# Adding the two halves of an attention result in memory: a tuned hybrid block kernel with accumulating transfers and a new order of units and steps

## The chip, the cores and the metric

The kernel runs on one core of a Trainium2 chip. The core has five engines with instruction queues of their own: TensorE (PE in the profile, with its weight loads shown as PEld), VectorE (DVE), ScalarE (ACT), GpSimd (POOL) and SyncE (SP). Sixteen DMA engines move data between memory and the core's SBUF. SP issues transfers through one hardware queue (q1 in the profile), GpSimd through a software queue (q0). The metric is the device time of one execution in microseconds, lower is better.

## The reference

One decoder layer over a sequence of 2048 tokens with model width 1024, in float32:

```python
h = rms_norm(x, norm_g)
u = jnp.einsum('bsd,dc->bsc', h, w_in)          # 8704 columns
v_c, b_c, c_c, z_c, q, k, v, z_a, gate_logits = jnp.split(u, SPLIT_POINTS, axis=-1)

y_c = b_c * causal_depthwise_conv(c_c * v_c, conv_w)     # width 3
y_c = y_c * jax.nn.silu(z_c)
y_a = jnp.einsum('bsc,cd->bsd', y_c, w_conv_out)

q = rms_norm(q.reshape(b, s, 16, 64), q_norm_g)
k = rms_norm(k.reshape(b, s, 4, 64), k_norm_g)
o = sliding_window_attention(q, k, v, sinks) * jax.nn.silu(z_a)   # window 128
y_b = jnp.einsum('bsc,cd->bsd', o, w_attn_out)

g_a, g_b = jnp.split(jax.nn.sigmoid(gate_logits + gate_b), 2, axis=-1)
merged = g_a * y_a + g_b * y_b
return x + jnp.einsum('bsd,de->bse', merged, w_out)
```

The attention result `o` has 1024 channels per token: 4 key heads, 4 query heads for each of them, 64 channels for each query head. It meets the gate `silu(z_a)` before its own projection.

## The kernel before

The sequence is worked in two halves ("tiles") of T = 1024 tokens, t = 0 and t = 1, channels on the 128 partitions and tokens along the free dimension. After both halves comes the last projection.

**Units.** A unit makes 256 output channels for the 1024 tokens of a half. It is the generator `sunit`: a block product of 2 x 2 by Winograd's scheme with seven products (`product`, L446) instead of eight. Every product is 12 matmuls of 128 x 128 by 128 x 512: each float32 operand is split into a high and a low part of the type that TensorE multiplies faster, and high x high, high x low and low x high are summed. The sums and differences of the weights and of the operands that the scheme needs are made by VectorE and ScalarE. A unit's name says what it makes: `q`, `k`, `v`; `cv` (C and V of the convolution branch), `b`; `ga`, `gb` (the merge gates); `z`, `za` (the gates of the two branches); `ya`, `yb` (the branches' own projections); `o` (the last one). Two units can run interleaved as a pair.

**Ticks.** The program is written out in order by hand. `run` advances one tick per product. `put(n, f)` registers a step for tick n; when that tick is reached, the step's instructions are written into the queues behind the product. A tick is thus a place in every engine's order, not a time: each engine takes its own instructions in that order and waits where an operand or a buffer is missing. A half counts 7 ticks for a unit and 14 for a pair. In the first half the key and value products take ticks 1 to 16, the `z` units begin at 186, the `za` units at 214, the `ya` pairs at 242.

**Attention.** A half has 32 rounds, one for each of 4 key heads and 8 blocks of 128 tokens, at the places in `AT0` and `AT1`. A round at place n loads queries and keys (n - 5), makes the scores in two PSUM banks of their own (`ps_s`), the exponentials (n + 1) and their norm (n + 2), turns the probabilities round through memory (`att_flip`, `att_back`), masks the two key blocks with GpSimd's affine selects (L1042, `att_low`, n + 10), and multiplies with the values (`att_values`, L1059, n + 13). The product `po` is a PSUM tile [128, 512]. Its upper and lower 64 partitions hold two halves of the same sums. In `att_out` (n + 14) ScalarE copies one half of `po` into a tile `o`, crosswise between partition halves (L1071); in `att_sum` (n + 15) VectorE adds the other half from PSUM (an `add`, recorded at L236), and SP stores the 128 x 256 result into `od[t]`, memory laid out as [8, 128, 1024]: channel group, channel in the group, token (L1079).

**The gates.** `fin_z` ends the `z` and `za` units. For each of the four pieces of a unit it loads 128 channels x 512 tokens of the branch's result (`load`, L1219: from `yd` for `z` into `zin`, from `od` for `za` into `zain`), ScalarE makes SiLU of the piece (L1229), VectorE multiplies it into the loaded tile, and the product is stored, with its sums and differences, for the `ya` and `yb` units (L1155 to L1163, L1236). `Z_AHEAD` says how many ticks ahead of its piece a load stands on SP.

**Next half.** `h_prep`, called ahead of the `z` units of the first half, makes the operands of the second: `x_roots` (L575) turns the roots of the token norms into rows with TensorE transposes, into a bank of the pool `ps_m` that holds also `po` and other small tiles; then GpSimd loads x, VectorE scales it, and the results are stored. `H_AT` gives the places. `w_prep` with `W_AT` does the like for the last weights. `load_set` loads what was stored, pair by pair, ahead of the units that use it.

**Buffers.** Nearly all tiles of up to 128 x 512 come from one pool of 19 slots (`big`); a tile's slot is free again when its last reader is done. Weights come through 4 raw tiles and 8 finished ones. `ps_m` has 3 PSUM banks, `ps_s` one tile of two banks.

Of the kernel before, what the change touches and what calls it, by code (L numbers as in the profile page):

```python
# [8 lines left out]
F32 = mybir.dt.float32  # L9
# [3 lines left out]
ALU = mybir.AluOpType  # L13
# [35 lines left out]
COL_GA, COL_GB = 6656, 7680  # L49

# [8 lines left out]

ORDER = (1, 5, 6, 2, 7, 3, 4)  # L60
# [13 lines left out]
AT1 = [  # L74
    41, 48, 54, 58, 67, 72, 75, 78, 81, 84, 88, 94, 98, 105, 109, 115, 119, 123, 126, 129, 132, 136,
    139, 142, 146, 150, 153, 157, 161, 164, 168, 174]
# [4 lines left out]
def block_kernel(  # L81
# [54 lines left out]
    od = [dram.tile([KC, P, T], F32, name=f"od{t}") for t in range(NT)]  # L136
# [434 lines left out]
    def x_roots(t, q, rs):  # L571

        pt = mbank(f"ptr{t}_{q}")
        for b in range(HB):
            nc.tensor.transpose(pt[:, b, :], rs[:, b : b + 1].to_broadcast([P, P]), ident)  # L575
# [488 lines left out]
    def att_out(t, j, b, po):  # L1064
        pov = po.rearrange("p (h e s c q) -> p h e s c q", h=2, e=2, s=2, c=2)
        o = slot([P, 2, P], F32, f"o{t}_{j}_{b}")
        parts = []
        for e in range(2):
            own, oth = HALVES[e], HALVES[1 - e]
            ov = o[own].rearrange("p c (h s q) -> p h s c q", h=2, s=2)  # L1070
            nc.scalar.copy(ov, pov[oth, :, e])  # L1071
# [140 lines left out]
    def fin_z(t, j, src, nm, key, to, at_of, eng):  # L1212
# [4 lines left out]
        def load(i, q):  # L1217
            o = got[i, q] = slot([P, H], F32, f"{nm}in{t}_{j}_{i}_{q}")
            nc.sync.dma_start(o, src[2 * j + i, :, hs(q)])  # L1219
# [120 lines left out]
    def h_prep(t, n0):  # L1340
# [4 lines left out]
        def roots(q):  # L1345
            rb[q] = x_roots(t, q, st["rt"][q])
# [32 lines left out]
    for t in range(NT):  # L1379
# [6 lines left out]
        def two(key, c0, t, j0):  # L1386
            paired.update((len(plan), len(plan) + 1))
            for j in range(j0, j0 + 2):
                at_((key, t, j), c0 + j * UC)

        if t == 0:
            for i in range(2):
                plan.append(("R", wkv[i * H : (i + 1) * H], ("kv", i)))
        else:
            two("ga", COL_GA, t, 0)
            at_(("k", t), COL_K)
            at_(("v", t), COL_VV)
        for j in range(NKV):
            at_(("q", t, j), COL_Q + j * UC)
            if t == j == 0:  # L1400
                plan[-1] = ("P",) + plan[-1][1:]
        for k in range(KC):
            s(("cv", t, k), (w_in2, COL_C + k * P), (w_in2, COL_V + k * P))
            if k % 2:
                at_(("b", t, k // 2), COL_B + (k // 2) * UC)
        for j in range(2 if t else 0, NJ):
            at_(("ga", t, j), COL_GA + j * UC)
        for j in range(NJ):
            at_(("gb", t, j), COL_GB + j * UC)
        for j in range(NJ):  # L1410
            at_(("z", t, j), COL_Z + j * UC)
        for j in range(NJ - 2):
            at_(("za", t, j), COL_ZA + j * UC)
        two("za", COL_ZA, t, NJ - 2)
        for key, w in (("ya", w_co), ("yb", w_ao)):
            for j in range(NJ):
                if j % 2 == 0:
                    paired.update((len(plan), len(plan) + 1))
                s((key, t, j), (w, j * UC), (w, j * UC + P))
# [92 lines left out]
    put(2, lambda: stats(0, 0))  # L1512
    put(2, lambda: stats(0, 2))
    put(2, lambda: roots(0))
    put(6, lambda: turned(0))
    put(7, lambda: stats(1, 0))
    put(7, lambda: stats(1, 2))
    put(8, lambda: roots(1))
    put(12, lambda: turned(1))
    put(4, lambda: plain_op(0, 1))  # L1520
    put(5, lambda: plain_op(2, 1))
    put(5, lambda: plain_op(4, 1))
    put(5, lambda: plain_op(6, 1))
    put(5, lambda: plain_op(1, 1))
    put(4, lambda: plain_op(3, 1))
    put(6, lambda: plain_op(5, 1))
    put(6, lambda: plain_op(7, 1))
    put(6, lambda: norm_l(0, 0, st))
    put(7, lambda: norm_l(0, 2, st))
    put(8, lambda: norm_l(0, 4, st))  # L1530
    put(6, lambda: norm_l(0, 6, st))
    put(9, lambda: norm_l(0, 1, st))
    put(8, lambda: norm_l(0, 3, st))
    put(7, lambda: norm_l(0, 5, st))
    put(6, lambda: norm_l(0, 7, st))
    put(9, lambda: form(0, 1, 0, st))
    put(15, lambda: form(0, 1, 1, st))
    put(8, lambda: form(0, 1, 2, st))
    put(14, lambda: form(0, 1, 3, st))
    put(12, lambda: norm_r(0, 0, st))  # L1540
    put(15, lambda: norm_r(0, 2, st))
    put(15, lambda: norm_r(0, 4, st))
    put(15, lambda: norm_r(0, 6, st))
    put(15, lambda: form(0, 8, 0, st))
    put(15, lambda: form(0, 8, 1, st))
    put(17, lambda: form(0, 8, 2, st))
    put(16, lambda: form(0, 8, 3, st))
    put(15, lambda: first_sum(0, st))
    put(16, lambda: first_sum(1, st))
    put(19, lambda: first_sum(2, st))  # L1550
    put(16, lambda: first_sum(3, st))
    put(16, lambda: form(0, 5, 0, st))
    put(17, lambda: form(0, 5, 1, st))
    put(20, lambda: form(0, 5, 2, st))
    put(17, lambda: form(0, 5, 3, st))
    put(13, lambda: norm_r(0, 1, st))
    put(15, lambda: norm_r(0, 3, st))
    put(12, lambda: norm_r(0, 5, st))
    put(14, lambda: norm_r(0, 7, st))
    put(19, lambda: second_sum(0, st))  # L1560
    put(17, lambda: second_sum(1, st))
    put(21, lambda: second_sum(2, st))
    put(19, lambda: second_sum(3, st))
    put(23, lambda: form(0, 6, 0, st))
    put(18, lambda: form(0, 6, 1, st))
    put(22, lambda: form(0, 6, 2, st))
    put(21, lambda: form(0, 6, 3, st))
    put(10, lambda: form(0, 2, 0, st))
    put(11, lambda: form(0, 2, 1, st))
    put(14, lambda: form(0, 2, 2, st))  # L1570
    put(9, lambda: form(0, 2, 3, st))
    put(20, lambda: third(1, st))
    put(16, lambda: third(3, st))
    put(22, lambda: third(5, st))
    put(21, lambda: third(7, st))
    put(26, lambda: form(0, 7, 0, st))
    put(22, lambda: form(0, 7, 1, st))
    put(24, lambda: form(0, 7, 2, st))
    put(27, lambda: form(0, 7, 3, st))
    put(23, lambda: t4(0))  # L1580
    put(22, lambda: t4(1))
    put(21, lambda: t4(2))
    put(23, lambda: t4(3))
    put(15, lambda: form(0, 3, 0, st))
    put(17, lambda: form(0, 3, 1, st))
    put(17, lambda: form(0, 3, 2, st))
    put(16, lambda: form(0, 3, 3, st))
    put(29, lambda: form(0, 4, 0, st))
    put(24, lambda: form(0, 4, 1, st))
    put(26, lambda: form(0, 4, 2, st))  # L1590
    put(29, lambda: form(0, 4, 3, st))
    KV_AT = {"p": (8, 9, 17, 19), "v": (8, 11, 19, 36), "r": (14, 32), "b": (29, 25, 39, 39)}
# [54 lines left out]
    for t in range(NT):  # L1647
# [3 lines left out]
        if t > 0:  # L1651
            paired_units([(("ga", t, j), ops, fin_g(t, 0, j)) for j in range(2)])
        a0 = t0 + (14 if t else 0)
        attention(t, [a0 + n for n in (AT0, AT1)[t]])
        if t > 0:
            run(sunit(("k", t), ops, fin_k(t)))
            run(sunit(("v", t), ops, fin_v(t)))
        for j in range(NKV):
            if t == j == 0:
                run(qunit(("q", t, j), ops, fin_q(t, j)))  # L1660
            else:
                run(sunit(("q", t, j), ops, fin_q(t, j), t == 0 and j < Q_TWO))
        for k in range(KC):
            run(sunit(("cv", t, k), ops, fin_cv(t, k, ys)))
            if k % 2:
                run(sunit(("b", t, k // 2), ops, fin_b(t, k // 2, ys)))
        if t + 1 < NT:
            h_stats(t + 1, tick[0] + 2)
        for j in range(2 if t else 0, NJ):
            run(sunit(("ga", t, j), ops, fin_g(t, 0, j)))  # L1670
        for j in range(NJ):
            run(sunit(("gb", t, j), ops, fin_g(t, 1, j)))
        if t + 1 < NT:
# [88 lines left out]
```

## Time and profile before

| | |
|---|---|
| runs | 1908.94, 1909.58, 1904.54 us; median 1908.94 |
| profiled execution | 1909.62 us, span 1907.9 us, granted clock 0.999 |
| busy | PE 1888.2, DVE 1591.0, ACT 1002.2, POOL 658.3 us |
| instructions | 28039 |
| DMA | 426.36 MB, 243141 packets, mean 223 GB/s |

The span runs from the first to the last instruction. Busy is the time in which at least one instruction of an engine was at work; matmuls overlap each other by more than a third, so a group's mean of 390 ns is not its step of 227 ns. "A <- B: t, n, m" in a list of waits means that A waited for B t us in all, n times, m us at the longest. A transfer's time "to landing" runs from its issue to its completion. SPq and POOLq stand for the engines' queues; a transfer that waits for a buffer waits there, with everything behind it on the same queue.

### The profile page before, as it was taken

To read this page: it belongs to the slowest core of one execution; us is meant where nothing else is said; L and a number is where in the kernel's file an instruction comes from. 1 tells how busy PE (TensorE), PEld (TensorE's weight loads), DVE (VectorE), ACT (ScalarE), POOL (GpSimd) and SP (SyncE) were. 2 spreads that over 40 slices of the span, in tenths; PEclk is the share of its full clock that TensorE was granted. 3 is DMA by queue.
4 is the path that set the end of the run, shared out by engine and by line. 5 is a ranking of instruction groups with operands and counts; after the bars stand their busy time and mean duration, and the time that the engine had idled before them with its cause. 6 is when DMAs were issued, how large, how long until landed. Compare 5 with 4: busy or idle time off the path is not lost.

```text
span 1907.9 us, 28039 instructions
## 1 busy us (share of the span) xinstructions
PE 1888.2 (99%) x8654; PEld 1566.9 (82%) x8654; DVE 1591.0 (83%) x2708; ACT 1002.2 (53%) x1990; POOL 658.3 (35%) x958
## 2 busy tenths in 40 slices
PE   9999999999999999999999999999999999999999
PEld 7778888888888888878887788888888888888887
DVE  7989899899887889887579989989888879887654
ACT  7655544567666345345445645555666436434321
POOL 1372444355665111121056344534665311111000
PEclk9999999999999999999999999999999999999999
DMA  8385554579876878999368556557887769989653
GB/s 305 98 221 161 174 169 149 170 236 289 246 233 213 281 263 307 322 291 303 113 185 200 159 166 194 162 174 211 245 251 225 268 218 349 331 263 279 227 174 111
DMA packets 243141, 426.36 MB, mean 223 GB/s; under 512 B 32240, under 2 KB 106992, under 8 KB 242992
## 3 DMA queue, kind: packets, MB, share of 16 engines
q1 hardware_dynamic: 202848, 314.13, 49.9%
q0 software_dynamic: 40000, 110.41, 20.3%
q8 instruction: 69, 1.13, 0.2%
q14 instruction: 80, 0.66, 0.1%
q10 hardware_dynamic: 144, 0.03, 0.0%
HBM read 278.43 MB, written 146.01 MB: 222 GB/s over the span
## 4 chain that ended last, share of the span: by engine, by line
PE 83%; DVE 6%; DMA 5%; issue 3%; POOL 2%; ACT 1%; SPq 0%; DVEq 0%; POOLq 0%; ACTq 0%
PE Y L446 28%; PE Vcv L446 4%; PE Xcv L446 4%; PE Xgb L446 2%; PE Xz L446 2%; PE Vz L446 2%; PE Vgb L446 2%; PE Xo L446 2%; PE Xza L446 2%; PE Vo L446 2%; PE Vza L446 2%; PE po L1059 2%; PE Xb L446 2%; PE Vb L446 2%; PE Xga L446 2%
## 5 line engine op out<-in xcount | busy, mean ns | idle before, releaser
L1021 POOL DMA_DIRECT2D x<-fd x256 | 139.7, 552 | 92.6 <-DMA fd<-f 60.3
L1042 POOL TENSOR_SCALAR_AFFINE_SELECT xh<-xh 64x512 fp32r<-64x512 f32 x64 | 69.3, 1082 | 141.6 <-DVE xl L236 98.7
L1014 POOL DMA_DIRECT2D fd<-f x64 | 36.9, 577 | 222.1 <-DVE f L236 180.6
L994 ACT ACTIVATE p<-s,st,rq 128x128 f32<-128x128 f32 x256 | 112.8, 449 | 0.0
L446 PE MATMUL Xcv<-oph,wcv_ah 128*128 128x512 f32 x256 | 79.4, 391 | 0.0
L1042 POOL TENSOR_SCALAR_AFFINE_SELECT xl<-xl 64x512 fp32r<-64x512 f32 x64 | 66.6, 1040 | 4.4
L1269 POOL DMA_DIRECT2D md<-thyb x32 | 27.5, 874 | 100.7 <-DVE thyb L236 95.9
L1042 POOL TENSOR_SCALAR_AFFINE_SELECT yp<-xl 64x512 fp32r<-64x512 f32 x64 | 57.4, 897 | 3.1
L1042 POOL TENSOR_SCALAR_AFFINE_SELECT yp<-yp 64x512 fp32r<-64x512 f32 x64 | 55.3, 864 | 4.2
L328 ACT CAST wcv_sh<-wcv_raw 128x1024 fp32r<-128x1024 f32 x16 | 16.8, 1053 | 74.3 <-DVE wcv_raw L236 68.9
L446 PEld LDWEIGHTS Xcv<-oph,wcv_ah 128*128 128x128 f32 x256 | 47.5, 188 | 9.5
L236 DVE TENSOR_TENSOR o<-po,o 64x256 f32<-64x256 f32 x128 | 53.4, 417 | 1.2
L816 POOL DMA_DIRECT2D q2d<-q_h x64 | 44.2, 690 | 26.4 <-ACT q_h L811 18.8
L236 DVE SCALAR_TENSOR_TENSOR y<-u,cols,y 128x512 f32<-128x512 f32 x64 | 50.5, 789 | 3.1 <-ACT y L1108 1.8
L236 DVE TENSOR_TENSOR opa<-ina,opa 128x512 fp32r<-128x512 f32 x56 | 36.2, 686 | 18.5 <-ACT opa L263 18.2
L991 ACT ACTIVATE st<-st 128x4 f32<-128x4 f32 x64 | 13.1, 205 | 72.4 <-DVE st L236 71.9
L994 ACT ACTIVATION_READ_ACCUMULATOR p<-s,st,rq 128x1 f32 x256 | 50.6, 198 | 0.0
L816 POOL DMA_DIRECT2D q2d<-q_l x64 | 44.1, 689 | 17.6 <-DVE q_l L236 8.7
L236 DVE TENSOR_TENSOR p<-p,st 128x512 f32<-128x512 f32 x64 | 47.4, 741 | 3.2
L1071 ACT COPY o<-po 64x256 f32<-64x256 f32 x128 | 47.0, 367 | 6.0 <-PE po L1059 3.7
L446 PE MATMUL Xcv<-oph,wcv_al 128*128 128x512 f32 x128 | 49.9, 389 | 0.0
L236 DVE TENSOR_TENSOR opc<-inc,opc 128x512 fp32r<-128x512 f32 x56 | 36.1, 686 | 14.4 <-ACT opc L263 14.3
(761 smaller groups left out, 6653.5 us busy)
## 6 DMA issues: line engine op xcount, KB each, us to landing
wcv_raw<-in_w_in SPq DMA_DIRECT2D x32, 512.0 KB, 3.9
q<-q2d SPq DMA_DIRECT2D x64, 256.0 KB, 4.3
v<-vd SPq DMA_DIRECT2D x128, 128.0 KB, 3.6
fd<-f POOLq DMA_DIRECT2D x64, 256.0 KB, 3.5
x<-fd POOLq DMA_DIRECT2D x256, 64.0 KB, 3.1
gd<-th SPq DMA_DIRECT2D x64, 256.0 KB, 3.1
wq_raw<-in_w_in SPq DMA_DIRECT2D x16, 512.0 KB, 5.1
q2d<-q_h POOLq DMA_DIRECT2D x64, 128.0 KB, 4.5
```

Source lines behind the costliest of these rows:

```text
L236: r = f(*args, **kw)
L328: return (lambda: nc.scalar.copy(hi, src), lambda: vec.tensor_tensor(out=lo, in0=src, in1=hi.bitcast(F32), op=ALU.subtract))
L446: nc.tensor.matmul(ps, lhsT=w[:, j, :], rhs=b[:, m, :], start=start and j == 0 and i == 0, stop=j == KP - 1 and i == 2, skip_group_check=n ...
L816: nc.gpsimd.dma_start(q2d[t][j][half, q * 2 * HB : (q + 1) * 2 * HB, i, e, :], src[HALVES[e]].bitcast(F32).rearrange("p (b x) -> p b x", x ...
L991: nc.scalar.activation(out=st[:, 3], in_=st[:, 2], func=AF.Exp)
L994: nc.scalar.activation(out=p[:, i, :], in_=sg[:, i, HD : 3 * HD], func=AF.Exp, bias=st[:, 1, i : i + 1], scale=rv[:, i // 2, i % 2 : i % 2 ...
L1014: nc.gpsimd.dma_start(fd, f)
L1021: nc.gpsimd.dma_start(x[QUADS[k]], src[k])
L1042: nc.gpsimd.affine_select(out=d4, in_=s4, pattern=[[0, 2], [-32 * sg, 2], [0, G], [-sg, 32]], compare_op=ALU.is_gt if prev else ALU.is_ge, ...
L1059: nc.tensor.matmul(po[:, cs], lhsT=v2[:, kind, :], rhs=xx[:, :, h * HD : (h + 1) * HD], start=h == 0 and n == 0, stop=n == 2, skip_group_c ...
L1071: nc.scalar.copy(ov, pov[oth, :, e])
L1269: nc.gpsimd.dma_start(md[t][k, :, hs(q)], m, accum_op=ALU.add)
```

## The change

The change has four parts.

1. **Attention result.** `att_out` now copies both halves of `po` into a tile `o` of [128, 2, 2, 128], each on its own partitions, two copies of [128 x 256]. VectorE adds nothing. `att_sum` stores the lower 64 partitions through SP into `od`, and `ADD_WAIT` = 2 ticks later GpSimd issues a transfer of the upper 64 partitions that adds to the same bytes. `od` is laid out anew: [4 key heads, 64 channels, 2 (e), 2 (c), 1024 tokens]. The gate's load reads 128 channels out of it with the order of dimensions e, channel, token.
2. **Roots.** For the second half both transposed rows of roots go into one tile of the scores' pool `ps_s` instead of two banks of `ps_m`; they stand 5 ticks later.
3. **Order of units.** It is given by two lists of names, `SEQ0` and `SEQ1`. The units are the same, as are the pairs.
4. **Places.** Steps at the start, some attention rounds, the first group of `H_AT` and of `W_AT` and `Z_AHEAD` (2 to 1) are placed anew.

```diff
+OP_X = [-1, 2, 2, 6, 7, 7, 8, 12]
+OP_P = [5, 4, 5, 4, 5, 6, 5, 6]
...
+SEQ0 = (
+    "q0 q1 q2 q3 cv0 cv1 cv2 cv3 b0 cv4 cv5 b1 b2 cv6 cv7 b3 gb1 ga0 gb2 ga1 gb0 ga2 ga3 gb3 z0 "
+    "z1 z2 z3 za0 za1 za2+za3 ya0+ya1 ya2+ya3 yb0+yb1 yb2+yb3")
+SEQ1 = (
+    "ga0+ga1 k v q0 q1 q2 cv0 q3 cv1 cv2 b0 cv3 ga3 b1 cv4 cv5 b2 cv6 cv7 gb1 b3 ga2 gb2 gb3 "
+    "gb0 z0 z1 z2 z3 za0 za1 za2+za3 ya0+ya1 ya2+ya3 yb0+yb1 yb2+yb3")
...
-Z_AHEAD = 2
+Z_AHEAD = 1
...
-H_AT = (11, 26, 66, 80)
-W_AT = [15, 33, 67, 84]
+H_AT = (16, 26, 66, 80)
+W_AT = [18, 33, 67, 84]
+ADD_WAIT = 2
...
-    51, 56, 61, 66, 72, 78, 82, 87, 93, 99, 103, 108, 113, 119, 123, 127, 130, 135, 139, 142, 146, 149,
-    153, 156, 160, 163, 167, 170, 174, 177, 181, 184]
+    51, 56, 62, 66, 72, 78, 82, 87, 93, 99, 103, 108, 113, 119, 123, 127, 130, 135, 139, 142, 146, 149,
+    153, 156, 160, 163, 166, 170, 174, 177, 181, 184]
...
-    od = [dram.tile([KC, P, T], F32, name=f"od{t}") for t in range(NT)]
+    od = [dram.tile([NKV, HD, 2, 2, T], F32, name=f"od{t}") for t in range(NT)]
...
     def att_out(t, j, b, po):
         pov = po.rearrange("p (h e s c q) -> p h e s c q", h=2, e=2, s=2, c=2)
-        o = slot([P, 2, P], F32, f"o{t}_{j}_{b}")
-        parts = []
+        o = slot([P, 2, 2, P], F32, f"o{t}_{j}_{b}")
         for e in range(2):
-            own, oth = HALVES[e], HALVES[1 - e]
-            ov = o[own].rearrange("p c (h s q) -> p h s c q", h=2, s=2)
-            nc.scalar.copy(ov, pov[oth, :, e])
-            parts.append((ov, pov[own, :, e]))
-        return o, parts
-
-    def att_sum(t, j, b, got):
-        o, parts = got
-        for ov, pv in parts:
-            add(ov, pv, ov)
-        nc.sync.dma_start(
-            od[t][2 * j : 2 * j + 2, :, b * P : (b + 1) * P].rearrange("c p q -> p c q"), o)
+            nc.scalar.copy(o[:, e].rearrange("p c (h s q) -> p h s c q", h=2, s=2), pov[:, :, e])
+        return o
+
+    def att_sum(t, j, b, o):
+        to = od[t][j, :, :, :, b * P : (b + 1) * P].rearrange("d e c q -> d (e c) q")
+        nc.sync.dma_start(to, o[LH].rearrange("p e c q -> p (e c) q"))
+        put(tick[0] + ADD_WAIT, lambda: nc.gpsimd.dma_start(to, o[UH].rearrange("p e c q -> p (e c) q"), accum_op=ALU.add))
...
-            nc.sync.dma_start(o, src[2 * j + i, :, hs(q)])
+            nc.sync.dma_start(o, src(2 * j + i, q))
...
-            rb[q] = x_roots(t, q, st["rt"][q])
+            if q == 0:
+                rb["banks"] = ps_s.tile([P, 2, HB, P], F32, tag="s", name=f"ptr{t}")
+            rb[q] = x_roots(t, q, st["rt"][q], rb["banks"][:, q])
...
+            elif key == "z":
+                fin = fin_z(t, j, lambda k, q: yd[t][k, :, hs(q)], "z", ("c", t), ycd[t], at_of, nc.sync)
+            elif key == "za":
+                fin = fin_z(t, j, lambda k, q: od[t][k // 2, :, :, k % 2, hs(q)].rearrange("d e q -> e d q"), "za", ("a", t), ocd[t], at_of, nc.gpsimd)
```

More of the change, by code (lines that the diff above doesn't have):

```diff
@@ L1384, in at_ @@
             s(key, (w_in2, c0), (w_in2, c0 + P))
[L1386 to L1389, printed above, removed]
         if t == 0:
@@ L1393, in block_kernel @@
                 plan.append(("R", wkv[i * H : (i + 1) * H], ("kv", i)))
[L1394 to L1419, printed above, removed]
+        for word in (SEQ0, SEQ1)[t].split():
+            both_ = word.split("+")
+            for name in both_:
+                if len(both_) > 1:
+                    paired.add(len(plan))
+                key, j = name.rstrip("0123456789"), int(name[-1]) if name[-1].isdigit() else None
+                if key in ("ya", "yb"):
+                    w = w_co if key == "ya" else w_ao
+                    s((key, t, j), (w, j * UC), (w, j * UC + P))
+                elif key == "cv":
+                    s((key, t, j), (w_in2, COL_C + j * P), (w_in2, COL_V + j * P))
+                elif j is None:
+                    at_((key, t), COLS[key])
+                else:
+                    at_((key, t, j), COLS[key] + j * UC)
+                if t == 0 and name == "q0":
+                    plan[-1] = ("P",) + plan[-1][1:]
     for n in range(S // P // 2):
@@ L1567, in block_kernel @@
[L1567 to L1592, printed above, removed]
+    for n, f in zip(OP_X, (
+            lambda: stats(0, 0), lambda: stats(0, 2), lambda: roots(0), lambda: turned(0),
+            lambda: stats(1, 0), lambda: stats(1, 2), lambda: roots(1), lambda: turned(1))):
+        put(n, f)
@@ new lines, in block_kernel, with forms, each, rights @@
+    for c in (0, 2, 4, 6, 1, 3, 5, 7):
+        put(OP_P[c], lambda c=c: plain_op(c, 1))
+    for c in (0, 2, 4, 6, 1, 3, 5, 7):
+        put(OP_L[c], lambda c=c: norm_l(0, c, st))
+    def forms(i):
+        for j in range(KP):
+            put(OP_F[KP * i + j], lambda j=j: form(0, FORMS[i], j, st))
+    def each(i, f):
+        for j in range(KP):
+            put(OP_S[KP * i + j], lambda j=j: f(j))
+    def rights(p):
+        for j in range(KP):
+            put(OP_R[2 * j + p], lambda c=2 * j + p: norm_r(0, c, st))
@@ L1593, in block_kernel @@
+    forms(0)
+    rights(0)
+    forms(1)
+    each(0, lambda j: first_sum(j, st))
+    forms(2)
+    rights(1)
+    each(1, lambda j: second_sum(j, st))
+    forms(3)
+    forms(4)
+    each(2, lambda j: third(2 * j + 1, st))
+    forms(5)
+    each(3, t4)
+    forms(6)
+    forms(7)
+    KV_AT = {"p": OP_K[:4], "v": OP_K[4:8], "r": OP_K[8:10], "b": OP_K[10:]}
     kv = KV()
@@ L1663, in block_kernel @@
[L1663 to L1666, printed above, removed]
-        if t + 1 < NT:
[L1668 to L1673, printed above, removed]
-            h_prep(t + 1, tick[0])
-        else:
-            w_prep(tick[0])
@@ new lines, in block_kernel @@
+        if t + 1 < NT:
+            h_stats(t + 1, tick[0] + STATS_AT)
+        for word in (SEQ0, SEQ1)[t].split():
+            n = tick[0] + 1
+            if word == "z0":
+                (h_prep if t + 1 < NT else w_prep)(*((t + 1,) if t + 1 < NT else ()), tick[0])
+            if word == "za2+za3":
+                load_set(("c", t), n, opa)
+            if word == "ya2+ya3":
+                load_set(("a", t), n, opb)
+            if word == "yb2+yb3":
+                load_set(("h", t + 1) if t + 1 < NT else ("w", 0), n, x_state(t + 1)["ops"])
+            names = word.split("+")
+            if len(names) > 1:
+                paired_units([
+                    unit_of(name, lambda e, i=i, n=n: n + 2 * e + i) for i, name in enumerate(names)])
+            elif t == 0 and word == "q0":
+                run(qunit(("q", 0, 0), ops, fin_q(0, 0)))
+            else:
+                run(sunit(*unit_of(word, lambda e, n=n: n + e)))
```

123 lines of the change are left out of this document (32 added, 91 removed).

## The prediction

> **What bounds the kernel now.** I read the page first: busy times and the chain that ended last. Then the stretches by stage, then who TensorE (PE) waited for, then the rows of the instructions and transfers that the diff names.
>
> ```profile
> span 1907.9 us, 28039 instructions
> ...
> PE 1888.2 (99%) x8654; PEld 1566.9 (82%) x8654; DVE 1591.0 (83%) x2708; ACT 1002.2 (53%) x1990; POOL 658.3 (35%) x958
> ...
> PE 83%; DVE 6%; DMA 5%; issue 3%; POOL 2%; ACT 1%; SPq 0%; DVEq 0%; POOLq 0%; ACTq 0%
> ```
>
> TensorE is the bound: it idles 1907.9 - 1888.2 = 19.7 us in all. The change leaves every matmul in place, so what it can win lies inside those 19.7 us; what it can lose has no such limit. The stretches below (columns: length, busy time of PE, PEld, DVE, ACT, POOL with counts, clock, mean busy share of the 16 DMA engines, GB/s) say where the idle time is.
>
> ```profile
> 0.00:100.00 100.00, 93.96 (x411) 75.81 (x411) 86.28 (x173) 68.65 (x121) 29.34 (x56) 0.98 0.62 202
> 100.00:415.00 315.00, 313.43 (x1463) 261.06 (x1463) 285.53 (x531) 169.67 (x379) 137.53 (x199) 1.00 0.60 179
> 415.00:480.00 65.00, 63.99 (x309) 53.61 (x308) 60.22 (x143) 47.96 (x110) 38.34 (x54) 1.00 0.88 283
> 985.00:1310.00 325.00, 320.54 (x1488) 265.42 (x1487) 293.54 (x538) 180.72 (x403) 151.40 (x217) 1.00 0.63 181
> 1750.00:1908.00 158.00, 154.15 (x681) 127.32 (x679) 89.10 (x121) 42.13 (x59) 3.43 (x4) 1.00 0.55 174
> ```
>
> Start and tail hold 6.0 + 3.8 us. The stretches with attention in them (100 to 480 and 985 to 1310) hold 1.6 + 1.0 + 4.5 = 7.1 us; VectorE is 90% busy in them. PE's longest single waits:
>
> ```profile
> PE ptr L575 <- DVE rtok L569: 2.2, 1, 2.2
> PE Y L446 <- DVE Vcv L236: 2.1, 1, 2.1
> ...
> PE po L1059 <- POOL xl L1042: 1.4, 1, 1.4
> ```
>
> So 7.1 us is all that a lighter VectorE and better places could return there, and 2.2 us at the first roots.
>
> **The change, part by part.**
>
> ```profile
> L1269 POOL DMA_DIRECT2D md<-thyb x32 | 27.5, 874 | 100.7 <-DVE thyb L236 95.9
> ...
> L236 DVE TENSOR_TENSOR o<-po,o 64x256 f32<-64x256 f32 x128 | 53.4, 417 | 1.2
> ...
> L1071 ACT COPY o<-po 64x256 f32<-64x256 f32 x128 | 47.0, 367 | 6.0 <-PE po L1059 3.7
> ```
>
> and of the transfers (issues, KB each, median us from issue to landing):
>
> ```profile
> od<-o SPq DMA_DIRECT2D x64, 128.0 KB, 2.6
> ...
> zain<-od SPq DMA_DIRECT2D x32, 256.0 KB, 5.6
> ...
> md<-thyb POOLq DMA_DIRECT2D x32, 256.0 KB, 7.0
> ```
>
> VectorE loses 128 additions of 417 ns, 53.4 us. ScalarE keeps 128 copies, on 128 partitions instead of 64 with the same 256 elements each: 0. The PSUM bank comes free after the copy, one addition sooner. All this is beside PE. Its worth on the path is between 0 and the 7.1 us above; the waits there are shared between VectorE, ScalarE and GpSimd (POOL), so I take half, -3.5.
>
> The store keeps 128 KB on SP. New are 64 accumulating transfers on POOL. The nearest row is the accumulation into md, 0.874 us of POOL each: 64 x 0.874 = 56 us more in stretches where POOL is about 45% busy (151.40 of 325.00). Each waits for its store to land. The store is issued two ticks earlier; a tick is one product of 12 matmuls, 2.72 us by this row of the chain (24 matmuls):
>
> ```profile
> 693.87 5.44 PE Xza L446 x24
> ```
>
> Two ticks are 5.4 us against a landing of 2.6, so the usual wait is 0. Behind the waiting accumulation stand the next rounds' affine selects (L1042) and transfers, and PE's po products wait for those selects. I take 0; the dear end is the second rival. Nothing excludes a gain by the freer bank, which is in the -3.5. The slot of o is held until the accumulation has landed: 5.4 + 0.9 + 7.0 instead of 2.6, 10.7 us more, 64 times over some 700 us of attention stretches, about one slot of 19; taken as 0, at worst it delays SP's loads by the like of the first rival's small waits.
>
> The gated read of the attention result (zain<-od) is where I see the cost. Before, one read takes a [128 x 512] block whose 128 rows lie evenly in memory. After, the od layout is [4, 64, 2, 2, 1024], and the read walks "e d q": an outermost dimension of 2 (the halves e), then 64 rows, then 512 contiguous elements, into 128 partitions. How a transfer of such a shape is dealt out to the DMA engines no row of before shows, because every transfer there has at least 32 entries outermost on both sides, and all ran on 16 engines:
>
> ```profile
> DMA packets 243141, 426.36 MB, mean 223 GB/s; under 512 B 32240, under 2 KB 106992, under 8 KB 242992
> ...
> q1 hardware_dynamic: 202848, 314.13, 49.9%
> ...
> q10 hardware_dynamic: 144, 0.03, 0.0%
> ```
>
> Queue q10 carried one transfer, the constants: 128 rows and 16 more packets, one completion per engine. Of the 32240 short packets 128 are those rows, and the other 32112 are 16 for each of 2007 transfers. So the price has two ends. Dealt to 16 engines, the read costs what it costs now. Dealt by its outermost entries, it has two shares, and two engines carry all of it. The stage rows, from the first zain load's issue to its last use in each half of the sequence, and the loads themselves:
>
> ```profile
> 663.90:744.70 80.80, 80.46 (x355) 66.10 (x354) 70.03 (x100) 40.02 (x64) 15.77 (x30) 1.00 0.77 275
> 1531.00:1610.50 79.50, 79.50 (x352) 65.63 (x351) 68.34 (x97) 39.25 (x63) 14.29 (x27) 1.00 0.75 268
> ```
>
> One busy engine moves 275 / (16 x 0.77) = 22.3 GB/s here (268 / (16 x 0.75) gives the same). A 262144-byte read over 16 engines takes each 0.73 us; over two it takes each 5.87 us. A half has 16 such reads: 93.9 us of both engines instead of 11.7. That alone is longer than the stage. Other traffic keeps an engine busy for 0.77 x 80.8 - 11.7 = 50.5 us of the first stage and 0.75 x 79.5 - 11.7 = 47.9 us of the second. Three values:
> - nothing of it stands before the reads: 93.9 - 80.8 = 13.1 and 93.9 - 79.5 = 14.4, +27.5 us;
> - all of it: 63.6 + 62.3, +125.9 us;
> - the part on SP's own queue, 314.13 of 426.36 MB or 74%, which is served in the order of issue, stands in the way and POOL's does not: 93.9 + 37.3 - 80.8 = 50.4 and 93.9 + 35.4 - 79.5 = 49.8, +100 us.
>
> Between the 16-engine end (0) and these I take two engines, since two shares is what the read's own shape offers without regrouping it, and the third value, since the reads and three quarters of the traffic are one queue. The delay reaches PE: VectorE multiplies zain in its program order, and its additions for PE's next products stand behind. What slack there is, these rows show:
>
> ```profile
> 663.86 1.29 SPq L1219 DMA_DIRECT2D zain<-od  x1
> ...
> 665.87 2.70 SPq L1219 DMA_DIRECT2D zain<-od  x3
> ...
> 670.34 0.69 DVE L236 TENSOR_TENSOR zain<-zain,zas 128x512 f32<-128x512 f32 x1 [0.38 <-DMA zain<-od]
> ...
> 681.18 0.69 DVE L236 TENSOR_TENSOR zain<-zain,zas 128x512 f32<-128x512 f32 x1
> ```
>
> Four loads go out in 4.7 us and are used between 6.5 and 17.3 us after the first; on two engines they alone need 4 x 5.87 = 23.5. Already now the first use waits 0.38 us. With Z_AHEAD 1 each load stands one tick (2.7 us) later on SP, behind a store or a weight load more.
>
> [...]
>
> The rest. The roots of the next half go into the score banks: the same 8 transposes, at ticks 201 and 202 counted from the start, when the last scores (tick 185) are read; no PE wait on these roots is among those of before, so 0 (dear end: one bank wait like the 2.2 above). The h loads, five ticks later in their first group, and the w_out loads, three later, keep more than 60 ticks to the sets that read them: 0. The order of units keeps their number, and so PE's work; cv units between lighter ones spread VectorE's load (in the -3.5), while y tiles wait longer for their b unit, 8 of 19 slots instead of 4 before b0: from -7.1 with the gain above to a wait or two of 2.1, taken 0. Start steps move by one to three ticks: between -2.2 and +2.2, taken 0.
>
> Sum: 1909.6 (the profiled execution: 1907.9 and 1.7 around it) + 100 - 3.5 = 2006 us. The median of the runs, 1908.94, is 0.7 below that execution.
>
> **The rivals.**
> - *The read is spread over all 16 engines.* Place: the zain loads; then they land in about 5.6 us within the 6.5 to 17 of slack, and PE stays the bound. 1909.6 - 3.5 = 1906, between 1902.5 and 1912 (one VectorE wait of 0.4 per load in six). For it: nothing in the trace binds a transfer to its outermost dimension. Against: all of its 2007 transfers fit that rule as well. It decides if a load's landing stays under 6.5 us. Faster or no change.
> - *POOL becomes the late engine.* Accumulations wait for stores that land late, and hold back the affine selects. If one round in four costs PE what POOL's worst select did, 16 x 1.4 = +22: 1909.6 + 22 - 3.5 = 1928. For it: transfers in the busier stages, reads of 256 KB though, land later than two ticks, as the row below shows. Against: POOL is idle more than half of the attention stretches. It decides when stores land later than 5.4 us.
>
> ```profile
> thyb<-gd SPq DMA_DIRECT2D x32, 256.0 KB, 8.7
> ```
>
> **How the numbers follow.** Two engines 0.72, with its own range 1934 (+27.5 - 3.5) to 2036 (+125.9); spread 0.21; POOL 0.07. I put the first that high because both layouts of the read are known exactly, the stage has no room (0.77 busy), and the only way out is a regrouping that nothing shows. About 0.3% (5.7 us) is what a measurement of this kernel can tell from no change; the three runs of before span 5.0. Spread gives 0.09 faster, 0.10 the same, 0.02 slower; the others are slower. The range goes from 1903, which takes in two thirds of the spread case and POOL, to 2036: 0.14 + 0.07 + 0.65 = 0.86.
>
> **What would show it.** In the profile after: the count of packets under 512 B. The 64 new transfers add 64 x 16 = 1024; at two completions for each of 32 reads 448 are missing, 32816, while 33264 means 16 engines and the forecast is wrong. zain<-od landing at 12 us or more in the median against 5.6; VectorE waiting for zain by some 100 us in all, PE idle about 60 us in each of the two gate stages and ya beginning that much later; DMA share lower there than 0.77. VectorE busy 53 us less, POOL 56 us more. POOL waits on o's landing, and PE's waits for xl growing past 1.4 us, would show the second rival. Waits of 3 us each could also lower the granted clock, which is 0.98 in the first stretch with its waits and 1.00 in all others; then the loss is above my range.

## The result and the profile after

The changed kernel takes 2004.14 us in the median (2002.12 to 2004.89), the kernel before 1909.35. The ratio is 1.0499, 95% interval 1.0483 to 1.0514. Predicted were 2006 us. The page of the changed kernel, in the lines shown of before, with the group of VectorE's gate products and that of the new transfers:

```profile
span 2003.0 us, 27973 instructions
...
PE 1910.4 (95%) x8654; PEld 1581.5 (79%) x8654; DVE 1542.7 (77%) x2580; ACT 989.8 (49%) x1990; POOL 722.4 (36%) x1022
...
DMA packets 260100, 434.74 MB, mean 217 GB/s; under 512 B 32816, under 2 KB 123952, under 8 KB 259952
...
PE 69%; issue 14%; DMA 7%; DVE 5%; POOL 3%; ACT 1%; SPq 1%; POOLq 0%; DVEq 0%; ACTq 0%
...
L255 DVE TENSOR_TENSOR zain<-zain,zas 128x512 f32<-128x512 f32 x32 | 21.6, 691 | 108.8 <-DMA zain<-od 100.7
...
L1094 POOL DMA_DIRECT2D od<-o x64 | 67.1, 1056 | 21.5 <-ACT wz_ah L347 9.7
```

TensorE idles 92.6 us instead of 19.7, and its share of the chain fell from 83 to 69%. VectorE waited 100.7 us for the reads of the attention result, which before was 0.4 us. The count of packets under 512 B is 32816, the number that the prediction gave for reads on two engines.

Where the time went is seen in the stretches (columns as in the prediction). Of the kernel before, from the first za product to the first ya product, on to the first yb product, and from there to the za units of the second half and through its za and ya units:

```profile
655.50:731.80 76.30, 76.30 (x338) 62.98 (x337) 65.81 (x93) 35.47 (x54) 12.39 (x23) 1.00 0.74 266
731.80:809.50 77.70, 76.72 (x337) 62.83 (x336) 68.45 (x101) 35.48 (x55) 12.81 (x24) 1.00 0.89 319
809.50:1523.00 713.50, 707.16 (x3289) 588.04 (x3288) 598.84 (x1034) 395.23 (x831) 299.40 (x423) 1.00 0.69 210
1523.00:1599.30 76.30, 76.30 (x337) 62.99 (x336) 63.30 (x90) 35.87 (x54) 10.80 (x20) 1.00 0.73 260
1599.30:1675.50 76.20, 76.20 (x337) 63.09 (x337) 68.65 (x100) 35.94 (x57) 12.92 (x24) 1.00 0.91 329
```

The same five of the changed kernel:

```profile
653.70:757.10 103.40, 85.75 (x338) 68.29 (x337) 66.85 (x93) 35.27 (x55) 12.40 (x23) 0.90 0.55 196
757.10:859.80 102.70, 82.17 (x337) 65.93 (x336) 68.39 (x100) 35.22 (x55) 12.79 (x24) 0.88 0.72 251
859.80:1567.40 707.60, 705.50 (x3289) 589.11 (x3288) 572.65 (x968) 388.13 (x829) 331.88 (x455) 1.00 0.75 217
1567.40:1667.60 100.20, 82.22 (x338) 65.79 (x337) 63.66 (x89) 36.09 (x55) 10.78 (x20) 0.91 0.52 188
1667.60:1770.60 103.00, 82.05 (x337) 66.16 (x336) 69.78 (x102) 36.40 (x56) 12.63 (x24) 0.88 0.74 255
```

The four gate stretches grew by 27.1, 25.0, 23.9 and 26.8 us, 102.8 in all. The long stretch between them shrank by 5.9, the part ahead of them by 1.8. That is the whole difference of the spans, 95.1. In the gate stretches the engines' mean share of transfer time fell, from 0.74 to 0.55 in the first. That fits two busy engines of 16, with the others waiting.

How the waiting travels, SP's queue shows in part. The timeline of SP in the changed kernel (columns: start us, length us, engine, line, operation, tiles, count; one row takes together what follows without a gap):

```profile
662.32 13.16 SPq L1233 DMA_DIRECT2D zain<-od  x4
679.68 9.79 SPq L325 DMA_DIRECT2D wza_raw<-in_w_in  x2
690.85 14.80 SPq L1233 DMA_DIRECT2D zain<-od  x4
```

The same timeline cut at 666 us, which leaves the last two of the first four reads:

```profile
665.27 10.21 SPq L1233 DMA_DIRECT2D zain<-od  x2
```

In the kernel before three such reads left SP in 2.70 us. Here the first two go out by 665.27, and the third and the fourth hold SP 5.1 us each, with weights and stores behind them. The 32 issues are not alike. Of the kernel before and of the changed one (count, then shortest, median and longest issue in ns, first and last start in us):

```profile
L1219 SPq DMA_DIRECT2D zain<-od x32: 320/450/1734, 663.9 to 1601.8; - x32
L1233 SPq DMA_DIRECT2D zain<-od x32: 502/1322/9381, 662.3 to 1689.2; - x32
```

A load of another kind right behind such reads is held on SP too, as this one of an operand of the `ya` units:

```profile
742.02 5.53 SPq L1209 DMA_DIRECT2D inc<-ycd  x1
```

PE's waits in the changed kernel (engine, line and tile that waited, what released it: us in all, times, longest):

```profile
PE Vya L465 <- ACT zas L1243: 20.0, 2, 10.1
PE Y L465 <- ACT opc L282: 18.5, 2, 9.4
PE Y L465 <- DVE Vza L255: 13.7, 2, 7.7
PE Vza L465 <- DVE wza_sl L255: 13.6, 5, 6.1
PE Yza L465 <- DVE zas L255: 5.8, 2, 3.2
```

They reach PE in two ways. The three waits for VectorE (Vza, wza_sl and zas, 33.1 us) lie in the `za` stretches, and in VectorE's order the work that PE waits for stands behind a gate product that waits for its read. That holds for wza_sl also, whose name is that of a weight: its longest wait in the first half ended at 717.37, after a gate product that had waited 5.81 us for its read, until 714.88. The first two rows (38.5 us) lie in the `ya` stretches and come through ScalarE, which makes the operands opc out of loads that SP issues (tile inc). Its wait for these loads, before and after:

```profile
L263 ACT CAST opc<-inc 128x512 fp32r<-128x512 f32 x56 | 32.2, 618 | 9.3 <-DMA inc<-ycd 7.4 <-DMA inc<-sdc 1.9
L282 ACT CAST opc<-inc 128x512 fp32r<-128x512 f32 x56 | 32.7, 617 | 50.5 <-DMA inc<-ycd 27.6 <-DMA inc<-sdc 22.7
```

The 18.5 us come right behind such loads; ahead of the 20.0 us VectorE stood at a read as well, 10.34 and 10.48 us. Whether the loads were late by their places on SP or by the busy engines was not told apart.

### The profile page after: what moved, and what is told of

Its sections match the earlier page's. It is cut to its first block, busy times and chain, and to the rows that moved or that the text cites. A ratio compares the mean times of both kernels' runs of the same rounds, so it can differ in the third digit from the quotient of the medians.

```text
span 2003.0 us, 27973 instructions
## 1 busy us (share of the span) xinstructions
PE 1910.4 (95%) x8654; PEld 1581.5 (79%) x8654; DVE 1542.7 (77%) x2580; ACT 989.8 (49%) x1990; POOL 722.4 (36%) x1022
## 2 busy tenths in 40 slices
DMA packets 260100, 434.74 MB, mean 217 GB/s; under 512 B 32816, under 2 KB 123952, under 8 KB 259952
## 4 chain that ended last, share of the span: by engine, by line
PE 69%; issue 14%; DMA 7%; DVE 5%; POOL 3%; ACT 1%; SPq 1%; POOLq 0%; DVEq 0%; ACTq 0%
PE Y L465 24%; PE Vcv L465 4%; PE Xcv L465 4%; PE Xga L465 2%; PE Xb L465 2%; PE Vb L465 2%; PE Xo L465 2%; PE Vo L465 2%; PE po L1079 2%; PE Vga L465 2%; PE Xgb L465 2%; PE Vgb L465 2%; PE Xz L465 2%; PE Vyb L465 2%; PE Xyb L465 2%
## 5 line engine op out<-in xcount | busy, mean ns | idle before, releaser
L1041 POOL DMA_DIRECT2D x<-fd x256 | 144.5, 609 | 78.4 <-DMA fd<-f 23.7
L255 DVE TENSOR_TENSOR zain<-zain,zas 128x512 f32<-128x512 f32 x32 | 21.6, 691 | 108.8 <-DMA zain<-od 100.7
L1094 POOL DMA_DIRECT2D od<-o x64 | 67.1, 1056 | 21.5 <-ACT wz_ah L347 9.7
L282 ACT CAST opc<-inc 128x512 fp32r<-128x512 f32 x56 | 32.7, 617 | 50.5 <-DMA inc<-ycd 27.6
L1014 ACT ACTIVATION_READ_ACCUMULATOR p<-s,st,rq 128x1 f32 x256 | 51.3, 200 | 0.0
L1250 POOL DMA_DIRECT2D ocd<-zain x24 | 13.0, 540 | 100.4 <-DVE zain L255 100.1
L255 DVE TENSOR_TENSOR opa<-ina,opa 128x512 fp32r<-128x512 f32 x56 | 36.2, 687 | 16.8 <-ACT opa L282 16.8
```

Of the source, the lines that this page charges most:

```text
L255: r = f(*args, **kw)
L282: nc.scalar.copy(hi, src)
L1014: nc.scalar.activation(out=p[:, i, :], in_=sg[:, i, HD : 3 * HD], func=AF.Exp, bias=st[:, 1, i : i + 1], scale=rv[:, i // 2, i % 2 : i % 2 ...
L1041: nc.gpsimd.dma_start(x[QUADS[k]], src[k])
L1094: put(tick[0] + ADD_WAIT, lambda: nc.gpsimd.dma_start(to, o[UH].rearrange("p e c q -> p (e c) q"), accum_op=ALU.add))
```

## The experiments

The theory: the read with two outermost entries runs on two engines, and these have more to do than the stage is long. Rivals: the accumulations or the new order cost the time; or each read is merely late.

**The reads split in two.** The changed kernel, and only the gate's load differs:

```diff
-            nc.sync.dma_start(o, src(2 * j + i, q))
+            if nm == "z":
+                nc.sync.dma_start(o, src(2 * j + i, q))
+            else:
+                for e in range(2):
+                    nc.sync.dma_start(o[HALVES[e]], od[t][j, :, e, i, hs(q)])
```

> The changed kernel with each read of the attention result issued as two reads, one for each half e, of 64 rows by 512 elements: no read has an outermost dimension of 2 any more. Theory (the read with two outermost entries runs on two engines): the whole loss goes. Outside the za and ya stages the changed kernel is already 7.6 us shorter than the kernel before, so 1902 us (1898 to 1907); packets under 512 B 33776 (32240, 64 x 16 for the accumulations, 32 x 16 for the reads that are now two); no VectorE waits for zain above a few us in all. Rival (the accumulating transfers or the new order cost the time): the loss stays, 1990 us or more.

Measured: 1905.75 us, ratio 0.9979 (0.9970 to 0.9987) to the kernel before. The page's count of its packets:

```profile
DMA packets 261060, 434.75 MB, mean 228 GB/s; under 512 B 33776, under 2 KB 124912, under 8 KB 260912
```

The count is the one expected, and VectorE's gate products waited 1.4 us for their reads. With 32 more transfers and all accumulations in place the whole loss is gone, 98 us, and the four gate stretches together are as long as before (306.4 us against 306.5). The time is 4 us above the expected 1902, inside the band given.

**The read's shape alone.** The kernel before, with `GR` = 2 groups. Its stores are two transfers each, as well, 64 more in all:

```diff
-    od = [dram.tile([KC, P, T], F32, name=f"od{t}") for t in range(NT)]
+    GR = 2
+    od = [dram.tile([NKV, P // GR, GR, 2, T], F32, name=f"od{t}") for t in range(NT)]
...
+        R = P // GR
+        for g in range(GR):
+            nc.sync.dma_start(od[t][j, :, g, :, b * P : (b + 1) * P], o[g * R : (g + 1) * R])
...
+                nc.sync.dma_start(o, src[j, :, :, i, hs(q)].rearrange("r g q -> g r q"))
```

> The kernel before with one thing changed: the attention result lies in memory as in the changed kernel (rows, then 2 groups) and is stored by two transfers of 64 partitions, so that the gate's read has 2 outermost entries; additions on VectorE, order and places as before. Theory: the read's shape alone makes the loss, +100: 2005 us (1985 to 2025), packets under 512 B 32240 + 64 x 16 - 32 x 14 = 32816. Rival (accumulations or order): 1909 us (1904 to 1915).

Measured: 2010.03 us, ratio 1.0527 (1.0512 to 1.0541), +100.5 us. Its packets by the page:

```profile
DMA packets 243717, 426.36 MB, mean 212 GB/s; under 512 B 32816, under 2 KB 107568, under 8 KB 243568
```

And VectorE's wait for the reads (us in all, times, longest):

```profile
DVE zain L237 <- DMA zain<-od: 75.7, 20, 6.9
```

The four gate stretches grew by 100.2 us in all and the rest of the span stayed as it was, so the added stores cost nothing that shows. The shape of 32 reads makes the loss without an accumulation and in the old order. The rival that accumulations or order cost it falls.

**Four groups instead of two.** As above with `GR = 4`.

> As the run with the read's shape alone, but with 4 groups of 32 rows, so 4 outermost entries, stored by four transfers of 32 partitions. Theory (as many engines as outermost entries): four engines, 2.93 us for each read, 47 us of each of the four per half beside 37 us of other traffic in 81 us: +3 us in each half, 1915 us (1909 to 1935); packets under 512 B 32240 + 192 x 16 - 32 x 12 = 34928. Rival (reading rows out of their order in memory is slow on any number of engines): near 2005 us. Rival (accumulations or order): 1909 us.

Measured: 1944.93 us, ratio 1.0183 (1.0167 to 1.0200), +35.4. Its packets by the page:

```profile
DMA packets 245832, 426.39 MB, mean 219 GB/s; under 512 B 34928, under 2 KB 109680, under 8 KB 245680
```

The packet count is again the expected one: four outermost entries, four completions, so four engines by the theory. The time is not: I expected +6 and at most +26. The loss falls as the number of outermost entries grows, so slowness of the row order alone is excluded, but my sum for its size missed; more on that below. The run also has 192 more stores on SP, outside the gate stages. The stretches from the first `za` to the first `yb` product in each half tell the two apart:

```profile
658.90:830.50 171.60, 156.71 (x674) 126.46 (x673) 135.13 (x193) 70.02 (x109) 25.29 (x47) 0.99 0.76 263
1546.60:1714.60 168.00, 159.64 (x673) 129.81 (x672) 132.94 (x189) 72.04 (x110) 23.76 (x44) 0.96 0.78 268
```

They are 339.6 us long, 33.1 more than before; the rest of this profiled execution grew by 6.0. So most of the miss lies in the gate stages.

**The reads earlier.** The changed kernel with a distance of 5 ticks in place of 1 for the za reads.

```diff
-            put(at_of(e) - Z_AHEAD, lambda i=i, q=q: load(i, q))
+            put(at_of(e) - (Z_AHEAD if nm == "z" else ZA_AHEAD), lambda i=i, q=q: load(i, q))
```

> The changed kernel with the reads of the attention result four ticks earlier in the queue (or at the start of their unit, where that is later). Theory (two engines have more to do than the stage is long): earlier issue gains its own length once in each half at most, 4 x 2.72 = 11 us: 1982 to 2004 us, 1992 the likeliest. Rival (each read only lands a few us late): the waits for zain vanish, 1905 us.

Measured: 2008.78 us, ratio 1.0522 (1.0505 to 1.0538). Nothing was won; the time lies above the 1982 to 2004 expected. The timeline of SP in this run:

```profile
661.09 13.31 SPq L1234 DMA_DIRECT2D zain<-od  x4
```

The first read of a unit could move by two ticks only, to the start of its unit, and in time it moved from 662.32 to 661.09, since stores of the unit before stood ahead of it on SP. VectorE's wait for all reads did fall, from 100.7 to 41.6 us, and the time did not. So the rival of mere lateness falls, and an earlier place within the unit is no remedy; a place ahead of the unit was not tried.

**More work for PE in the same stage.** The changed kernel computes the first product of each za unit twice.

```diff
+        if key[0] == "za":
+            product(xb, u, 1, ops, True)
         product(xb, u, 1, ops, True)
```

> The changed kernel with the first product of each of the 8 za units computed twice (12 matmuls more in each, 8 x 2.72 = 21.8 us of PE work at full clock, more at half); the result is the same. Theory (in the za stages the two engines set the pace, and PE's lower clock there lies in the waits): 0 to 5 us above the changed kernel's ratio of 1.0499, 2004 to 2010 us. Rival (PE's own time, its 22 us at half clock among it, adds to the waits): 2026 us or more.

Measured: 2005.25 us, ratio 1.0503 (1.0488 to 1.0517), the changed kernel's within its interval. The stretches from the first za to the first yb product, of the changed kernel,

```profile
653.70:859.80 206.10, 167.91 (x673) 134.22 (x672) 135.25 (x192) 70.49 (x109) 25.19 (x47) 0.89 0.63 224
1567.40:1770.60 203.20, 164.27 (x673) 131.95 (x672) 133.44 (x190) 72.48 (x110) 23.41 (x44) 0.90 0.64 222
```

and of this run,

```profile
654.50:859.90 205.40, 174.03 (x721) 140.85 (x720) 135.78 (x193) 70.70 (x109) 25.94 (x48) 0.91 0.64 225
1567.20:1770.10 202.90, 174.31 (x722) 140.46 (x721) 133.06 (x189) 72.45 (x110) 23.80 (x44) 0.93 0.64 224
```

are equally long with 97 more matmuls recorded in them (96 were added). PE no longer sets the pace of the `za` units, where they were added. Its granted clock of 0.89, at which its matmuls are busy for longer (167.91 us for 673 of them, against 76.30 + 76.72 us for 675 at 1.00 in the kernel before), costs nothing on top there, because there was room for 96 more.

**The reads on GpSimd's queue.** As the run with earlier reads, with `eng.dma_start` for the za reads, `eng` being GpSimd.

> The run with earlier reads, but GpSimd issues the 32 reads instead of SP; their shape is as in the changed kernel. Theory (the loss is made by one queue that sends all its narrow reads to the same two engines and then stands): if GpSimd's queue puts each narrow read on other engines than the one before, the reads run beside each other and SP's loads are free of them: 1905 to 1925 us. If it uses the same two engines each time: 1990 us or more, as now. Rival (a narrow read is slow by itself wherever it runs, 6 us and more of waiting each): 1950 to 2000 us.

Measured: 1949.46 us, ratio 1.0210 (1.0192 to 1.0228). The time lies 0.5 us below the third case's range (single runs went from 1946.50 to 1952.66), but the waits of 6 us and more for each read, which that case names, are not there, as the last row below shows. So the time does not decide between the cases; the trace says more. Its packets by the page:

```profile
DMA packets 272836, 434.86 MB, mean 224 GB/s; under 512 B 47600, under 2 KB 138736, under 8 KB 272688
```

The transfers (issues, KB each, median us from issue to landing):

```profile
zain<-od POOLq DMA_DIRECT2D x32, 256.0 KB, 9.9
```

And its waits (us in all, times, longest):

```profile
POOL zain L1234 <- issue: 55.8, 9, 14.4
...
PE Y L466 <- DVE zas L256: 19.4, 2, 18.5
...
DVE zain L256 <- DMA zain<-od: 3.9, 1, 3.9
```

A narrow read lands after 9.9 us in the median, where a wide one of before took 5.6. VectorE waited for it once, 3.9 us, instead of 100.7 in all. So 59 us of the loss go when the same reads leave SP's queue (2008.78 to 1949.46). What is left lies in the four gate stretches, which are 45.6 us longer in all than before. GpSimd stood 55.8 us before these reads without a wait that the profile shows, once 14.4. By the profile the stores behind that one were late, VectorE waited 16.8 us until one of them had landed, and PE 18.5 us for VectorE. That this is the same holding as SP's is likely but not shown. On which engines these reads ran, no row tells. Each of these reads adds 448 short packets to the 33264 that 16 completions for each read would make ((47600 - 33264) / 32). By the bytes of the two pages (434.86 against 434.74 MB, for 47600 - 32816 = 14784 more short packets) they are of some 8 bytes each, an estimate.

**The rest of the change.** Order and places without accumulation: the changed kernel with the `att_out`, `att_sum`, `od` layout and gate read of the kernel before.

```diff
-    od = [dram.tile([NKV, HD, 2, 2, T], F32, name=f"od{t}") for t in range(NT)]
+    od = [dram.tile([KC, P, T], F32, name=f"od{t}") for t in range(NT)]
...
+        for ov, pv in parts:
+            add(ov, pv, ov)
```

> The changed kernel with the attention result added by VectorE, stored and read as in the kernel before: what is left is the order of units, the places and the roots in the score banks. Theory (the 4 us that the run with two reads gains come from VectorE's lighter load): 1909 us, ratio 1.000 within 0.002. Rival (they come from order and places): ratio 0.998, 1905.5 us.

Measured: 1904.60 us, ratio 0.9969 (0.9960 to 0.9979). The rival holds. Beside it the run with split reads (0.9979) has the same order and places and 46 us less of VectorE (1544.8 us busy against 1590.6), and is not faster.

The accumulation alone: the kernel before with the new `att_out`, `att_sum` and `od`, and the reads split in two.

```diff
-        for ov, pv in parts:
-            add(ov, pv, ov)
+        put(tick[0] + ADD_WAIT, lambda: nc.gpsimd.dma_start(to, o[UH].rearrange("p e c q -> p (e c) q"), accum_op=ALU.add))
```

> The kernel before with the attention result accumulated in memory as in the changed kernel and read by two reads of 64 rows; order, places and roots as before. Theory (the 4 us come from VectorE's lighter load): ratio 0.998, 1905.5 us. Rival (from order and places): ratio 1.000 within 0.002; if the accumulations hold GpSimd back, above 1.002.

Measured: 1910.39 us, ratio 1.0002 (0.9993 to 1.0011). VectorE is 49 us lighter (1542.0 us busy against 1591.0), and that is worth nothing that could be measured. This kernel, the next one and the one with the roots in the old banks do not compute the layer's values right, for a reason that stayed open. They do the same number of products, and are used for their times alone; what rests on this run is borne out by the pair just named, both of which compute them right.

The same with `ADD_WAIT = 6`:

> The run of the accumulation alone (ratio 1.000), with each accumulating transfer 6 ticks behind its store instead of 2. Theory (stores have landed after 2 ticks, GpSimd loses nothing by waiting): ratio 1.000 within 0.002. Rival (GpSimd waits for stores and holds PE back, which hides a gain by VectorE's lighter load): 0.998 or less; if the slot of o is what counts, held 4 ticks longer, 1.002 or more.

Measured: 1914.98 us, ratio 1.0028 (1.0019 to 1.0037). More distance brought no gain, so there is no sign that GpSimd's waiting at two ticks hid one. A result tile held longer is the third case expected, and the 0.3% fit it; that the slot is what costs them was not shown.

Old order of units at the new places: `SEQ0` and `SEQ1` in the order of the kernel before.

> The run of order and places without accumulation (ratio 0.997), with the two lists of units in the order of the kernel before; the places of the steps stay new. Theory (the new order of units makes the gain, most of it between the last projection of the first half and the za units of the second): the gain goes, ratio 0.999 to 1.003. Rival (the new places of the steps make it): 0.997.

Measured: ratio 0.9994 (0.9985 to 1.0003). New order at the old places of the steps (`OP_X` to `OP_K`, `AT0`, `AT1`, `H_AT`, `W_AT`, `Z_AHEAD` of the kernel before):

> The run of order and places without accumulation (ratio 0.997), with the step places of the kernel before (start, attention rounds, operand and weight loads, gate loads 2 ticks ahead); the order of units stays new. Theory (the order makes the gain): ratio 0.997 to 0.999. Rival (the places make it, or order and places only together): 1.000 or more, since attention rounds placed for the old order then fall on other units.

Measured: ratio 0.9978 (0.9969 to 0.9986). So the order of units makes most of the gain, which is 0.2 to 0.3% in all; the places alone make none that is clear of noise, and what they add to the order is within the intervals.

The roots back in two banks of `ps_m`, on the run of order and places:

> The run of order and places without accumulation (ratio 0.997), with the second half's roots turned in two banks of ps_m again, at the new places. Theory (the roots' place is worth nothing, since no PE wait on them is among those of before): ratio 0.997 within 0.002. Rival (the score banks keep PE from a wait): 0.999 or more.

Measured: ratio 0.9964 (0.9951 to 0.9978). As far as its time tells, the roots' place is worth nothing that could be measured.

The run of order and places without accumulation beats both kernels, the changed one by 5%; so does, by a little less against the kernel before, the changed kernel with split reads.

## Why the prediction was right, point by point

- **PE is the bound and can win little.** Right until the gate stages; there the narrow reads took the pace over, as the split reads and the doubled product show together.
- **The read runs on two engines.** Right, as far as completions tell: the packet count (32816) shows two for each read, where the kernel before has 16 for each transfer (32112 for 2007), and the loss came and went with the read's shape in both kernels. That one completion stands for one engine is my reading of 16 completions beside 16 engines; no row names the engines themselves. Nor does a run show that all 32 reads went to the same two engines, as the 93.9 us of a half take it. What the runs show is a count that follows the outermost entries (32816 packets for two, 34928 for four) and a loss that goes with it (100.5 and 35.4 us).
- **+100 us.** Measured: +100.5 for the shape alone, 98 when it is taken out of the changed kernel. Its terms are less sure than the sum. I had 5.87 us for a read and 74% of the other traffic in its way. If the pace of a read is what SP's first rows give, 5.1 us (10.21 for two; an estimate, since single issues ran from 0.5 to 9.4 us), a half has 16 x 5.1 = 81.6 us; with all of the other traffic that makes 81.6 + 50.5 - 80.8 = 51.3 and 81.6 + 47.9 - 79.5 = 50.0, +101. So two errors may have cancelled, and that the sum came within 2 us of the time is in part luck. Neither version gives the four-engine run: by 5.1 us and all traffic it would be +20, by 5.87 us and all traffic +32, measured +35.4. That SP's queue is served in the order of issue, as the third value takes it, no run shows; how much other traffic stands in the way is open.
- **The delay reaches PE through VectorE.** VectorE's wait of about 100 us came as named (100.7), but it is only part of the way. For a landing of 12 us or more the profile has no row of these reads. In the `ya` stretches PE waited for operands whose loads stood on SP with the narrow reads (ScalarE waited 50.3 us for them, 9.3 before), which the prediction did not have. In the run with earlier reads VectorE's wait fell by 59.1 us and the time stayed, so that wait alone does not set the loss. I expected PE idle for about 60 us in each pair of gate stages; idle were 206.1 - 167.9 = 38.2 and 203.2 - 164.3 = 38.9, and the rest was matmuls at a lower clock. The warning that a lower clock would bring a loss above the range was wrong: the clock fell, and in the `za` units that cost nothing, as shown.
- **-3.5 us for a lighter VectorE and a better order.** The size was right (split reads: -3.8 against the kernel before), the source was not: the accumulation gives nothing, at the old order or at the new; the order of units gives most of it.
- **56 us of GpSimd, waits 0.** The accumulations took 67.1 us, 1.056 us each instead of the 0.874 of the row I used, and GpSimd waited for their stores 5.6 us in four places. The rival of a late GpSimd did not come.
- **ScalarE's copies, 0.** Right: 376 ns each in the median on 128 partitions, 368 on 64.
- **The slot of o, taken as 0.** Right at two ticks; at six the kernel was 0.3% slower, perhaps by the slot.
- **Roots, 0.** Right, by the time of the run with the old banks.
- **VectorE 53 us less.** 48.3 us by the two pages.

## What to carry to other kernels

Reads of the same 256 KB cost this kernel nothing extra, about 35 or about 100 us by the number of entries in their outermost dimension (128, 4 or 2): count those entries before a layout is changed, and check in the trace how many completions SP's transfers make, which here followed that number at once (32816 packets under 512 B with two entries, 34928 with four, as expected). When a load is late, find out first whether it stands behind other work: here an earlier place within the unit did not help, and splitting each read in two, the same bytes in more transfers, took the whole loss away. An engine that is 83% busy is not for that reason on the path: 49 us less of VectorE bought nothing, a different order of the same units some 4 us, and 6 with the new places.

## What the hardware did that I had not expected

SP does not always hand a narrow read over and go on: of the first four the third and the fourth held it for 5.1 us each (13.16 us for four, against 2.70 for three wide ones), and over all 32 an issue took up to 9.38 us, against 1.73 before. Loads of other shapes behind them were held too (5.53 us for the one shown), so that these were late as well. On GpSimd's queue the same reads landed in 9.9 us and brought 448 short packets each. PE's granted clock fell to between 0.88 and 0.91 in the waiting stages, and in the `za` units this was free, since 97 more matmuls recorded did not lengthen them.
